# Moving one pool mix ahead of a pool gate's product in the mixer's TensorE order

## The chip, the cores and the metric

The kernel runs on one core of one Trainium2 chip. The metric is the device time of one execution in microseconds, the median over runs. Five engines work side by side: TensorE (PE, with its weight loads PEld), VectorE (DVE), ScalarE (ACT), GpSimd (POOL) and SyncE (SP), which issues most of the transfers.

## The reference, cut to what matters

One block of a network for 256 tokens of width 2048: a feed-forward part (SwiGLU, inner width 5632), a mixer, and a second feed-forward part, each with a norm before and after and a residual. All is float32. The change lies in the mixer:

```python
def _hybrid_mixer(u, ...):
    p = u @ w_in
    z_a, z_b, g_a, g_b = jnp.split(p, IN_SPLITS, axis=-1)
    y_a = _rwkv7_branch(z_a, ...) @ w_proj_a
    y_b = _pool_branch(z_b, pool_w, pool_scale) @ w_proj_b
    m = jax.nn.sigmoid(g_a) * y_a + jax.nn.sigmoid(g_b) * y_b
    return m @ w_out

def _pool_branch(z, pool_w, pool_scale):
    ...                      # four groups of 256 channels, windows 2, 4, 8, 16
    mixed = pooled - zf      # window mean less the value itself
    y = jnp.einsum('bsgc,gcd->bsgd', mixed, pool_w.astype(jnp.float32))
    y = y.reshape(bsz, seq, POOL_WIDTH) * pool_scale.astype(jnp.float32)
    return y.astype(z.dtype)
```

A *pool mix* is one of the four products `mixed[g] @ pool_w[g]` (256 tokens, 256 by 256). A *pool gate* is 512 of the 2048 columns of `g_b`, with its sigmoid.

## The kernel before, in words

**Products.** Each float32 product is made of three passes over halves: a weight tile w is cast to wH on ScalarE (L342), and the rest wL = w - wH is made on VectorE (L343); the activations are halved in the same way, and `mm3` (L364, with the matmuls L366 to L368) adds wH with the high half, wL with the high half, and wH with the low half. Weights come in by SP's queue (`get_w`, L328) in tiles of 128 by 1024 elements, 512 KB, into four buffers, and the halves go into a ring of five pairs. A full tile feeds two steps of k for both halves of the tokens, 12 matmuls of 512 columns. The weights of a pool mix are one tile of 128 by 512 (256 KB), which feeds 12 matmuls of 256 columns (L976).

**The mixer's groups.** TensorE's order in the mixer is written out by hand as a chain of generators:

- `tok_g` (L887) is a product of 512 columns over the 16 (or 8) tiles of k, tokens on the partitions; it holds two of the four PSUM banks of the pool `mm`, one for each half of the tokens (h = 0 and 1), which take turns at every k. `gb_g(c)` is a pool gate made in that way; its two banks are emptied by ScalarE's sigmoid (L1594) into `sgb`. `z_g(hf, ...)` makes columns of r, k or v for one half of the recurrence's heads; ScalarE empties them at L1135. `pb_g(c)` is the product of the pool branch with w_proj_b, which multiplies into `sgb` (L1663); `ga_g(c)` is a gate of the other branch.
- `mix_g(g)` is a pool mix, by `pool_mix` and `ch_g` (L963): channels on the partitions, one bank of the same pool (`mc`). It is emptied in four steps that follow each other, ScalarE (L1789), VectorE (L1790), and the same again for the second half of the channels, into `yb`.
- `chain(hf)` is the recurrence itself for half the heads: many small matmuls, with work on all engines between them. `weave` fills the time between its steps with matmuls of the generator `rest`.

`seq` runs a list of such groups. Before a group empties its banks it lets the next group do its first step (`prime`), so that TensorE has work.

**What sets the order.** In the mixer only TensorE's order is the written one. What ScalarE, VectorE, GpSimd and SP do, and in which order, is set by the framework's scheduler from the program's dependencies, its own model of time and priorities; casts, low halves and evictions have a raised priority (`BOOST`). The banks and the larger buffers are given out in the order in which the scheduler sees them come free. The two feed-forward parts have a planner of their own (`Plan`), on which the change does not touch.

**Around the change.** A first list runs w_in's columns for the LoRA parts, the two halves of the pool columns, k and v of the first half of the heads, `mix_g(0)`, `mix_g(1)`, and r (`z_g(0, 4)`). Then the list of `rest` begins, as the filler of `chain(0)`: the gate `gb_g(1)`, then `mix_g(2)` and `mix_g(3)`, then k for the second half of the heads (`z_g(1, 1)`). The inputs of all four mixes (`mix[g]`, by `pool_window`) are made with the pool columns, well ahead of all of these. In the profile the window of the change is 840 to 895 us.

Of the kernel before, what the change touches and what calls it, by code (L numbers as in the profile page):

```python
# [260 lines left out]
class Block:  # L261
# [1322 lines left out]
    def mixer(s, prm, uT, rs, resid, emit, gpost, reload):  # L1584
# [7 lines left out]
        def ev_sig(dst):  # L1592
            def ev(h, ps):
                nc.scalar.activation(out=dst(h), in_=ps, func=AF.Sigmoid, scale=rs[h])  # L1594
            return ev
# [40 lines left out]
        def z_g(hf, part=0):  # L1636
            for nme, zc in ((("k", 1), ("v", 2), ("r", 0)), (("k", 1),),
                            (("v", 2), ("r", 0)), (("v", 2),), (("r", 0),))[part]:
                z[hf][nme] = s.unit((P, 4, S), F32, "z" + nme)
                c0 = zc * W + hf * 512  # L1640
                yield from s.across(w_in, c0, at, rs, lambda v: s.shift(
                    v, c0 // P, [z[hf][nme][:, i] for i in range(4)]), scratch(hf))
# [12 lines left out]
        def gb_g(c):  # L1655
            sg = sgb[c] = [s.tmp("sgb"), s.tmp("sgb")]
            yield from s.tok_g(w_in, GB + c * 512, at, NKD, ev_sig(lambda h: sg[h]))

        def pb_g(c):
            sg = sgb[c]  # L1660

            def ev_pb(h, ps):
                nc.vector.tensor_tensor(out=sg[h], in0=ps, in1=sg[h], op=ALU.mult)  # L1663
                nc.gpsimd.dma_start(out=msp[c, :, h], in_=sg[h])
            yield from s.tok_g(prm["w_proj_b"], c * 512, at_b, NKW, ev_pb)
# [4 lines left out]
        def scratch(hf=0):  # L1670
            n = next(turn)
            if hf:
                return [s.unit(p="sc") for _ in range(3)]
            return [s.R[(3 * n + i) % 15] for i in range(3)]
# [7 lines left out]
        def mix_g(g):  # L1682
            yield from s.pool_mix(g, mix[g], prm["pool_w"], pT)
# [3 lines left out]
        def ga_g(c):  # L1687
            sg = s.unit((P, 2, 512), F32, "sga")
            sga.append(sg)
            yield from s.tok_g(w_in, GA + c * 512, at, NKD, ev_sig(lambda h: sg[:, h]))  # L1690
# [28 lines left out]
        pair = s.pair_g(prm["w_proj_a"], (0, 512), at_a, NKW, 4, (ev_pa(0), ev_pa(1)))  # L1719

        def rest():
            yield from s.seq([gb_g(1), mix_g(2), mix_g(3), z_g(1, 1), pb_g(0), pb_g(1), z_g(1, 3), z_g(1, 4), gb_g(2), pb_g(2), gb_g(3), pb_g(3)]
                             + [ga_g(c) for c in range(4)])
            for t in pair:
                if t is None:
                    return
                yield t
# [9 lines left out]
        with s.tc.manual_schedule(engines={mybir.EngineType.PE}):  # L1737
            fill = rest()
            for _ in s.seq([s.across(w_in, 3 * W, at, rs, ev_l, scratch(), 288),  pool_g(0), pool_g(1), z_g(0, 1), z_g(0, 3), mix_g(0), mix_g(1), z_g(0, 4)], fill):
                pass  # L1740
            for hf in range(2):
                s.pre_at = PRE_AT[1 + hf]
                weave(chain(hf), fill)
            for _ in fill:
                pass
# [494 lines left out]
```

## Time and profile before

| | before |
|---|---|
| median of 3 runs | 2007.59 us (2006.14 to 2008.42) |
| the profiled execution | 2004.61 us |
| its span, first to last instruction | 2002.9 us |
| TensorE matmuls, busy | 1990.1 us, 99% |
| VectorE, busy | 1815.1 us, 91% |
| ScalarE, busy | 1223.8 us, 61% |
| GpSimd, busy | 406.3 us, 20% |
| mean granted clock of TensorE | 0.998 |

Matmuls are pipelined and their ends are modelled, so the busy share of TensorE says that matmuls follow each other, not that it is at its peak. What a wait costs is read from the distance between the starts of matmuls.

### The profile page before, as it was taken

The page shows a single profiled execution, that of the slowest core. Times are in us where ns is not written, and L with a number is a line of the kernel's source. Part 1 is how long each engine was busy: PE and PEld are TensorE (multiplying, and loading weights), DVE is VectorE, ACT ScalarE, POOL GpSimd, SP SyncE. Part 2 cuts the span into 40 slices and gives each one's busy share as a digit, 9 for nine tenths or more (in the row PEclk, how much of TensorE's full clock was granted, in tenths as well). Part 3 has the DMA queues.
Part 4 walks back from the last instruction along what each step waited for, and adds up shares of the span by engine and source line. Part 5 has one row for each costly group of instructions (what it writes and reads, how often), then busy time and mean ns, then how long its engine had stood idle before and what let it go on. Part 6 is the DMA issues. An engine that isn't in the chain of part 4 may idle for free.

```text
span 2002.9 us, 29049 instructions
## 1 busy us (share of the span) xinstructions
PE 1990.1 (99%) x9903; PEld 1644.6 (82%) x9903; DVE 1815.1 (91%) x2468; ACT 1223.8 (61%) x1631; POOL 406.3 (20%) x745
## 2 busy tenths in 40 slices
PE   9999999999999999999999999999999999999998
PEld 7888888888888888878788788888888888888886
DVE  7999999999999957789689678989999999999997
ACT  7566665666666566675466435575666666666653
POOL 2000001574100114402320111010000115650000
PEclk9999999999999999999999999999999999999999
DMA  9868896987778777757456547769688889897774
GB/s 346 277 208 262 253 265 216 282 269 229 236 223 261 263 202 212 209 164 215 148 170 188 168 159 258 267 227 297 216 248 268 240 271 272 265 265 220 239 255 169
DMA packets 253110, 470.79 MB, mean 235 GB/s; under 512 B 27299, under 2 KB 30752, under 8 KB 252960
## 3 DMA queue, kind: packets, MB, share of 16 engines
q1 hardware_dynamic: 213696, 400.37, 60.6%
q0 software_dynamic: 38976, 68.03, 15.0%
q8 instruction: 78, 1.28, 0.3%
q10 hardware_dynamic: 288, 0.52, 0.1%
q14 instruction: 72, 0.59, 0.1%
HBM read 443.88 MB, written 8.39 MB: 226 GB/s over the span
## 4 chain that ended last, share of the span: by engine, by line
PE 95%; DVE 2%; issue 1%; DMA 1%; ACT 0%; SPq 0%; DVEq 0%; POOLq 0%; POOL 0%; ACTq 0%
PE mm L366 25%; PE mm L368 25%; PE mm L367 25%; PE ms L368 5%; PE ms L367 5%; PE ms L366 5%; PE tr L1014 1%; DMA w<-in_w_out_dram 1%; PE pA L1967 0%; DVE wL L430 0%; DVE wL L681 0%; PE pU L2052 0%; PE pSa L2064 0%; DMA x<-in_x_dram 0%; PE pY L2087 0%
## 5 line engine op out<-in xcount | busy, mean ns | idle before, releaser
L366 PE MATMUL mm<-wH,xH 128*128 128x512 f32 (+1 forms) x2008 | 784.2, 391 | 1.1 <-ACT sgb L1594 0.6
L367 PE MATMUL mm<-wL,xH 128*128 128x512 f32 (+1 forms) x2008 | 779.5, 388 | 0.1
L368 PE MATMUL mm<-wH,xL 128*128 128x512 f32 (+1 forms) x2008 | 779.5, 388 | 0.0
L366 PEld LDWEIGHTS mm<-wH,xH 128*128 128x128 f32 x2008 | 377.1, 188 | 79.9 <-ACT sgb L1594 1.0
L368 PEld LDWEIGHTS mm<-wH,xL 128*128 128x128 f32 x2008 | 377.0, 188 | 78.7 <-DVE xL L1032 1.1
L367 PEld LDWEIGHTS mm<-wL,xH 128*128 128x128 f32 x2008 | 377.3, 188 | 76.2 <-DVE wL L343 0.9
L676 ACT CAST wH<-t 128x1024 fp32r<-128x1024 f32 x244 | 257.0, 1054 | 211.7 <-DVE t L668 97.3
L420 ACT CAST wH<-w 128x1024 fp32r<-128x1024 f32 x293 | 301.7, 1052 | 119.4 <-PE mm L368 98.3
L430 DVE TENSOR_TENSOR wL<-w,wH 128x1024 fp32r<-128x1024 f32 x293 | 349.8, 1217 | 19.3 <-ACT wH L420 17.7
L681 DVE TENSOR_TENSOR wL<-t,wH 128x1024 fp32r<-128x1024 f32 x244 | 293.0, 1216 | 2.4 <-ACT wH L676 1.4
L342 ACT CAST wH<-w 128x1024 fp32r<-128x1024 f32 (+2 forms) x184 | 188.8, 1029 | 173.8 <-PE mm L368 151.9
L343 DVE TENSOR_TENSOR wL<-w,wH 128x1024 fp32r<-128x1024 f32 (+2 forms) x184 | 217.4, 1188 | 84.0 <-ACT wH L342 82.5
L676 ACT CAST wH<-w 128x1024 fp32r<-128x1024 f32 x244 | 199.4, 836 | 119.2 <-PE mm L368 92.1
L681 DVE TENSOR_TENSOR wL<-w,wH 128x1024 fp32r<-128x1024 f32 x244 | 229.0, 949 | 0.1
L1057 POOL DMA_DIRECT2D x<-T x352 | 179.0, 568 | 146.4 <-DVE wL L681 45.6
L654 POOL DMA_DIRECT2D t<-in_ffn_up_dram x47 | 56.7, 1209 | 569.5 <-DVE wL L681 161.6
L367 PE MATMUL ms<-wL,sH 128*128 128x512 f32 x312 | 121.4, 389 | 0.0
L368 PE MATMUL ms<-wH,sL 128*128 128x512 f32 x312 | 121.4, 389 | 0.0
L366 PE MATMUL ms<-wH,sH 128*128 128x512 f32 x312 | 121.4, 389 | 0.0
L668 DVE TENSOR_TENSOR t<-w,t 128x512 f32<-128x512 f32 x122 | 83.2, 682 | 0.2
L664 DVE TENSOR_TENSOR t<-w,t 128x512 f32<-128x512 f32 x122 | 82.8, 683 | 0.1
L659 DVE TENSOR_TENSOR t<-w,w 128x1024 f32<-128x1024 f32 x62 | 75.3, 1217 | 3.8 <-DMA w<-in_ffn_down_dram 3.8
(353 smaller groups left out, 2308.0 us busy)
## 6 DMA issues: line engine op xcount, KB each, us to landing
w<-in_w_in_dram SPq DMA_DIRECT2D x128, 512.0 KB, 4.3
w<-in_ffn_down_dram SPq DMA_DIRECT2D x104, 512.0 KB, 6.3
w<-in_ffn_up_dram SPq DMA_DIRECT2D x94, 512.0 KB, 5.8
w<-in_ffn_gate_dram SPq DMA_DIRECT2D x92, 512.0 KB, 6.6
w<-in_ffn_gate_dram SPq DMA_DIRECT2D x168, 256.0 KB, 5.8
w<-in_ffn_down_dram SPq DMA_DIRECT2D x131, 256.0 KB, 5.0
w<-in_ffn_up_dram SPq DMA_DIRECT2D x117, 256.0 KB, 5.8
t<-in_ffn_up_dram POOLq DMA_DIRECT2D x47, 512.0 KB, 8.1
```

Of the source, the lines that this page charges most:

```text
L342: s.nc.scalar.copy(vH, v)
L343: s.nc.vector.tensor_tensor(out=vL, in0=v, in1=vH.bitcast(F32), op=ALU.subtract)
L366: nc.tensor.matmul(ps, aH, bH, start=start, stop=False, skip_group_check=seeded)
L367: nc.tensor.matmul(ps, aH, bL, start=False, stop=False, skip_group_check=seeded)
L368: nc.tensor.matmul(ps, aL, bH, start=False, stop=stop, skip_group_check=seeded)
L420: nc.scalar.copy(x["H"], x["v"])
L430: nc.vector.tensor_tensor(out=x["L"], in0=x["v"], in1=x["H"].bitcast(F32), op=ALU.subtract)
L664: V.tensor_tensor(out=v["t24"][:, 0], in0=v["a"][:, 0], in1=v["t13"][:, 1], op=ALU.add)
L668: V.tensor_tensor(out=v["t24"][:, 1], in0=v["b"][:, 1], in1=v["t24"][:, 0], op=ALU.add)
L676: nc.scalar.copy(H, src)
L681: V.tensor_tensor(out=L, in0=src, in1=H.bitcast(F32), op=ALU.subtract)
L1057: nc.gpsimd.dma_start(out=x[0][q * 32:q * 32 + 32, i], in_=src[i * 32:i * 32 + 32, q])
```

## The change

`mix_g(2)` moves to the front of the list of `rest`, ahead of the pool gate `gb_g(1)`. `mix_g(3)` stays behind the gate. The instructions are the same in kind and number.

```diff
         def rest():
-            yield from s.seq([gb_g(1), mix_g(2), mix_g(3), z_g(1, 1), pb_g(0), pb_g(1), z_g(1, 3), z_g(1, 4), gb_g(2), pb_g(2), gb_g(3), pb_g(3)]
+            yield from s.seq([mix_g(2), gb_g(1), mix_g(3), z_g(1, 1), pb_g(0), pb_g(1), z_g(1, 3), z_g(1, 4), gb_g(2), pb_g(2), gb_g(3), pb_g(3)]
                              + [ga_g(c) for c in range(4)])
```

## The prediction

> **What bounds the kernel now.** I read the page's busy shares first, then the waits of TensorE, the table by stage around the edited place, and last the timelines of TensorE, VectorE and ScalarE in that stage.
>
> ```profile
> span 2002.9 us, 29049 instructions
> ...
> PE 1990.1 (99%) x9903; PEld 1644.6 (82%) x9903; DVE 1815.1 (91%) x2468; ACT 1223.8 (61%) x1631; POOL 406.3 (20%) x745
> ...
> PE 95%; DVE 2%; issue 1%; DMA 1%; ACT 0%; SPq 0%; DVEq 0%; POOLq 0%; POOL 0%; ACTq 0%
> ```
>
> The last line is the chain that ended last: it is 95% matmul. A change of order adds no matmul, so it can only give back time in which TensorE stands. Where TensorE waits between 700 us and 1240 us (all of the mixer up to w_out) is this whole list:
>
> ```profile
> PE mm L366 <- ACT sgb L1594: 0.6, 1, 0.6
> PE pU L2052 <- DVE R L2077: 0.3, 1, 0.3
> ```
>
> One of its two rows lies at the edit. L1594 is the sigmoid that empties a gate's PSUM bank (gb_g, ga_g). The weight loads of TensorE, asked from 865 to 895 us, show a second kind of wait:
>
> ```profile
> PEld mm L367 <- DVE wL L343: 0.9, 2, 0.5
> ```
>
> So the low half of a weight tile (wL, L343 on VectorE) comes just too late twice. The table by stage (stretch, length, then busy us of PE, PEld, DVE, ACT and POOL, granted clock, DMA share, GB/s) says why:
>
> ```profile
> 850.00:860.00 10.00, 10.00 (x59) 8.64 (x59) 5.64 (x10) 7.70 (x13) 3.69 (x3) 1.00 0.78 221
> ...
> 870.00:880.00 10.00, 9.36 (x45) 7.30 (x44) 9.88 (x17) 7.79 (x15) 0.53 (x1) 1.00 0.29 74
> ```
>
> From 870 us VectorE is full (9.88 of 10) while TensorE is not (9.36); from 850 to 860 us VectorE has 4.36 us to spare. TensorE's timeline (start, length, instruction, and the wait in brackets):
>
> ```profile
> 839.97 0.39 PE L366 MATMUL mm<-wH,xH 128*128 128x512 f32 x1
> ...
> 868.23 0.28 PE L976 MATMUL mc<-mxT,wH 128*128 128x256 f32 x1
> ...
> 870.98 0.28 PE L976 MATMUL mc<-mxT,wH 128*128 128x256 f32 x1
> 871.10 0.40 PE L366 MATMUL mm<-wH,xH 128*128 128x512 f32 x1
> ...
> 871.57 0.40 PE L368 MATMUL mm<-wH,xL 128*128 128x512 f32 x1
> 872.55 0.51 PE L366 MATMUL mm<-wH,xH 128*128 128x512 f32 x1 [0.58 <-ACT sgb L1594]
> 872.89 0.40 PE L367 MATMUL mm<-wL,xH 128*128 128x512 f32 x1
> ...
> 877.00 0.39 PE L367 MATMUL mm<-wL,xH 128*128 128x512 f32 x1
> 877.23 0.39 PE L368 MATMUL mm<-wH,xL 128*128 128x512 f32 x1
> 877.45 0.39 PE L366 MATMUL mm<-wH,xH 128*128 128x512 f32 x1
> 877.90 0.50 PE L367 MATMUL mm<-wL,xH 128*128 128x512 f32 x1
> 878.24 0.39 PE L368 MATMUL mm<-wH,xL 128*128 128x512 f32 x1
> ...
> 890.52 0.39 PE L366 MATMUL mm<-wH,xH 128*128 128x512 f32 x1
> 890.87 0.50 PE L367 MATMUL mm<-wL,xH 128*128 128x512 f32 x1
> 891.21 0.40 PE L368 MATMUL mm<-wH,xL 128*128 128x512 f32 x1
> ```
>
> gb_g(1) begins at 839.97 and ends with the matmul before 868.23; mix_g(2) and mix_g(3) are the mc rows from 868.23 to 870.98, 24 matmuls in 871.10 - 868.23 = 2.87 us, so 1.44 us for each mix; z_g(1, 1) begins at 871.10. A steady step is 877.23 - 877.00 = 0.23 us. Longer steps are the waits: at 871.57, 0.98 - 0.23 = 0.75, and at 872.55, 0.34 - 0.23 = 0.11, together **0.86** (bank); at 877.45 and 877.90, 0.22 + 0.11 = **0.33** (wL); at 890.52 and 890.87, 0.12 + 0.11 = **0.23** (wL). That makes 1.42 us in the whole stage.
>
> **The bank wait.** In the program before, the four PSUM banks of the products go in the order in which they come free: gb_g(1) has banks 0 and 1, mix_g(2) bank 2, mix_g(3) bank 3, and z_g(1, 1) again 0 and 1. Its second half (h = 1) so needs the gate's second bank, which ScalarE empties last:
>
> ```profile
> 870.25 0.70 ACT L1594 ACTIVATE sgb<-mm,rs 128x512 f32<-128x512 f32 x1
> ...
> 871.80 0.69 ACT L1594 ACTIVATE sgb<-mm,rs 128x512 f32<-128x512 f32 x1
> ```
>
> Bank 0 is free at 870.95, bank 1 at 872.49; the matmul follows at 872.55.
>
> **The change, part by part.**
>
> *Matmuls of mix_g(2).* Twelve, 1.44 us, leave 868.23 and stand at 839.97. Nothing is added: z_g(1, 1) still begins at 871.10, since its matmul predecessors are the same set. One more border between 256- and 512-column groups arises (mix_g(2) and mix_g(3) no longer touch); the two steps behind such a border take 871.57 - 871.10 = 0.47 against 2 x 0.227, so it costs under 0.05 us, taken as 0.
>
> *Banks.* mix_g(2) takes the bank that is free longest at 839.97 (that of mix_g(0)), gb_g(1) then the two of z_g(0, 4), and mix_g(3) and z_g(1, 1) find mix_g(1)'s and mix_g(2)'s, both evicted long since, and for h = 1 the *first* bank of gb_g(1). That is needed at 871.10 + 3 x 0.23 = 871.79. If ScalarE keeps the sigmoid at 870.25, it is free at 870.95: no wait. The gate ends 1.44 us later than now, 869.67 plus the drain, which still is before 870.25. Term: -0.86. From the other side: had z_g(1, 1) to take both banks of the gate again, the need for the second at 871.79 would meet its release at 872.49, and the 0.86 stays.
>
> The gate's own start is new: at 839.97 + 1.44 = 841.41 and 842.09 it needs the banks of z_g(0, 4), the later of which is emptied here:
>
> ```profile
> 840.47 0.68 ACT L1135 ACTIVATE R<-mm,rs 128x512 f32<-128x512 f32 x1
> ```
>
> Free at 841.15, with 0.9 us in hand. Term 0.
>
> *Evictions of mix_g(2)* (two on ScalarE L1789, two on VectorE L1790, one after the other). VectorE's place now:
>
> ```profile
> 876.62 2.35 DVE L343 TENSOR_TENSOR wL<-w,wH 128x1024 fp32r<-128x1024 f32 x2
> 878.89 0.48 DVE L1790 SCALAR_TENSOR_TENSOR yb<-mc,cols,yb 128x256 fp32r<-128x256 f32 x1
> ...
> 888.81 0.48 DVE L1790 SCALAR_TENSOR_TENSOR yb<-mc,cols,yb 128x256 fp32r<-128x256 f32 x1
> ...
> 889.60 3.49 DVE L343 TENSOR_TENSOR wL<-w,wH 128x1024 fp32r<-128x1024 f32 x3
> ```
>
> By the order of tiles these two are mix_g(2)'s. Each holds VectorE for up to 0.48 us, so up to 0.96 us leave the full stage and go to 841 to 860, where 4.36 us are free in the second half. They stand ahead of the conversion at 889.60, whose first result the matmul at 890.87 waits for; with 0.96 less, the 0.23 there go, if TensorE arrives no earlier than now. They stand behind the conversion at 876.62, so the wait at 877.90 is not relieved by them. What their new place may cost: VectorE splits the LoRA weights there, and TensorE takes them soon after.
>
> ```profile
> 842.12 1.22 DVE L361 TENSOR_TENSOR wL<-w,wH 128x1024 fp32r<-128x1024 f32 x1 [0.23 <-ACT wH L360]
> 844.84 0.28 PE L1830 MATMUL pw<-lq,wL 128*128 128x256 f32 x1
> ```
>
> 1.50 us in hand. If both pairs went ahead of it, at worst in series on the two engines, 4 x 0.48 = 1.92: a loss of 0.4 at most. I take 0, since all four must meet one 1.2 us stretch for it.
>
> *Weight tile of mix_g(2).* Its transfer (256 KB, L328 on SP), its cast (L342) and its low half (L343, 128x512) move ahead of all eight tiles of gb_g(1), in the ring of five converted tiles too. The stream is far ahead there: gb_g(1)'s second tile is converted at 833.09 + 1.23 = 834.32 and first read at 842.91.
>
> ```profile
> 833.09 1.23 DVE L343 TENSOR_TENSOR wL<-w,wH 128x1024 fp32r<-128x1024 f32 x1 [1.49 <-ACT wH L342]
> 842.91 0.39 PE L367 MATMUL mm<-wL,xH 128*128 128x512 f32 x1
> ```
>
> That is 8.59 us; The mix's tile, half as wide, costs each engine no more than such a conversion, 1.23, so cover remains. It is the only transfer that the move issues: on SP's queue it passes eight of w_in, on POOL's none. At the other end the ring gets looser: a mix's tile holds a slot but feeds TensorE only 1.44 us, and two of them side by side shrink the reach of the ring just before 871.10. With one, the slot for z_g(1, 1)'s third tile (the one late at 877.90) comes free 2.72 - 1.44 = 1.28 us sooner (a full tile is 12 steps of 0.23). But VectorE converts that tile only at 876.62, 4 us after the sigmoids, behind work of the recurrence. So there are two ends. If those two lists stay, TensorE reaches 877.04 instead of 877.90 and waits the gained 0.86 for the same conversion. If the conversion moves up, the 0.33 goes as well.
>
> *Sum.* The ends are 0 and -1.42. I take the bank wait's **-0.9**: it is the one wait that the order itself touches, and I leave the two wL waits as they are, since one may grow and the other shrink by similar amounts. Against the profiled execution, 2004.61 (span 2002.9) becomes 2003.7. The median of the runs, 2007.59, lies 2.98 above it, so the forecast is **2006.7**. That is 0.05%; about 0.2%, or 4.0 us, is what a measurement of this kernel can tell from no change. Further on TensorE stands only in the 0.3 of the second row above, so a gain at 872 is carried along.
>
> **The rivals.**
>
> *A, the wait moves to wL.* Price as above: all of the bank gain is spent at 877.90, and only the relief at 890.87 is left, between -0.23 and 0: 2007.4. For it: VectorE at 9.88 of 10, and a conversion that is already the last to come. Against it: the slot that opens 1.28 us sooner.
>
> *B, the bank wait stays* because z_g(1, 1) is given both of the gate's banks, or ScalarE puts the first sigmoid after 871.79: 2007.6. Against: two banks are free longer. [...]
>
> *C, slower: the moved mix is evicted late.* Its bank is wanted by mix_g(3) or z_g(1, 1). If its last L1790 stays where it is now, at 888.81 + 0.48 = 889.29, z_g(1, 1) stands from 871.10, 18.2 us: 2025.8. It decides from 871.1 on. For it: the first two mixes, run just ahead of z_g(0, 4), 32 x 3 steps of 0.227 (21.8 us) before 839.97, so they end near 818.2. Their last eviction is
>
> ```profile
> 843.26 0.48 DVE L1790 SCALAR_TENSOR_TENSOR yb<-mc,cols,yb 128x256 fp32r<-128x256 f32 x1
> ```
>
> It ends at 843.74, 25.5 us later. Against it: that lag, from 841.4, ends at 866.9, still 4.2 before the need. The lists of ScalarE and VectorE are set anew by the framework's scheduler, so this rival stands for a poor new list too. The granted clock is 1.00 in both stage rows, through the wait of 0.75. [...]
>
> **How the numbers follow.** Forecast 0.50, A 0.22, B 0.12, C 0.13, and 0.03 for faster by over 0.2%, which the 1.42 us of waits here do not hold. Forecast, A and B all lie within 0.2%, so same is 0.84, slower 0.13. The range: down, the 1.42 us and the spread of the three runs below their median (2007.59 - 2006.14 = 1.45) give 2004.7. Up, the spread above it (0.83) and a mild form of C give 2010.5: for the latter I take 2.1 us, the longest wait that the evictions cause now:
>
> ```profile
> 879.41 0.47 ACT L1789 ACTIVATE yb<-mc,cols 128x256 fp32r<-128x256 f32 x1 [2.10 <-DVE yb L1790]
> ```
>
> **What the next profile would show.** Right: no wait of a matmul for L1594 near 872; mc rows near 840 and near 869.7 with 12 matmuls each; the moved L1790 before 860. Rival A: the step before 877.9 longer than 0.45. B: the L1594 row is still there. C: a wait of TensorE for L1790. The forecast is wrong in size if any wait over 1 us appears between 840 and 1240, since every instruction list but TensorE's is made anew for the whole kernel.

## The result and the profile after: 0.13% slower, nearly all of it at one place

| | before | after |
|---|---|---|
| median of 22 runs each | 2005.8 us (2004.84 to 2008.42) | 2008.46 us (2007.2 to 2010.52) |
| ratio after to before | | 1.0013, 95% interval 1.0007 to 1.0019 |
| span of the profiled execution | 2002.9 us | 2007.3 us |

The ratio makes 2.6 us (1.4 to 3.8). The forecast was a gain of 0.9; the change costs instead: little, but the whole interval lies above 1. The page after shows the same work as before:

```profile
span 2007.3 us, 29049 instructions
...
PE 1989.7 (99%) x9903; PEld 1643.1 (82%) x9903; DVE 1816.7 (91%) x2468; ACT 1223.9 (61%) x1631; POOL 407.8 (20%) x745
```

The number of matmuls is the same, so the loss is time in which TensorE stands. The waits of TensorE from 700 to 1240 us (waiting instruction, what it waits for, us in total, times, longest) were two rows before; now there are five, of which these are new:

```profile
PE mm L366 <- ACT wH L342: 1.5, 1, 1.5
PE mm L367 <- DVE wL L343: 0.9, 1, 0.9
PE pn L1877 <- issue: 0.5, 1, 0.5
...
PE pA L1967 <- ACT R L1959: 0.3, 1, 0.3
```

The row for L1594 (the sigmoid) of before is not among the five. The first two are one place, where mix_g(2) ends and gb_g(1) begins. TensorE's timeline after:

```profile
842.46 0.28 PE L976 MATMUL mc<-mxT,wL 128*128 128x256 f32 x1
842.58 0.28 PE L976 MATMUL mc<-mxT,wH 128*128 128x256 f32 x1
844.35 0.50 PE L366 MATMUL mm<-wH,xH 128*128 128x512 f32 x1 [1.49 <-ACT wH L342]
845.81 0.50 PE L367 MATMUL mm<-wL,xH 128*128 128x512 f32 x1 [0.95 <-DVE wL L343]
846.14 0.40 PE L368 MATMUL mm<-wH,xL 128*128 128x512 f32 x1
```

The reader takes the starts: 844.35 - 842.58 = 1.77 where a mix's step is 0.12; 845.81 - 844.35 = 1.46 and 846.14 - 845.81 = 0.33 where a step is 0.227. Above the steady steps that is 1.65 + 1.23 + 0.11 = **2.99 us**: the gate's first weight tile comes too late, first its cast, then its low half.

To count the whole change, three matmuls serve as marks in TensorE's timeline: the first of z_g(0, 4), the first of pb_g(1), and the last of the program. Before, then after:

```profile
818.18 0.40 PE L366 MATMUL mm<-wH,xH 128*128 128x512 f32 x1
...
914.21 0.40 PE L366 MATMUL mm<-wH,yb 128*128 128x512 f32 x1
...
1993.16 0.39 PE L368 MATMUL mm<-kH,xL 128*128 128x512 f32 x1
```

```profile
819.48 0.40 PE L366 MATMUL mm<-wH,xH 128*128 128x512 f32 x1
...
918.64 0.39 PE L366 MATMUL mm<-wH,yb 128*128 128x512 f32 x1
...
1997.57 0.39 PE L368 MATMUL mm<-kH,xL 128*128 128x512 f32 x1
```

From z_g(0, 4) to pb_g(1) it was 96.03 us and is 99.16; from there to the end 1078.95 and 1078.93. How steady such a distance is, the traces of four of the experiments below show: from pb_g(1) to the end, where their order is that of before, they have 1078.87 to 1078.92. So the change costs **3.1 us**, all within these 96 us. The spans differ by 4.4, but 819.48 - 818.18 = 1.30 of that arises before the change is reached, in the wait for the first input (TensorE's waits up to 60 us, before and after):

```profile
PE tr L1014 <- DMA x<-in_x_dram: 0.4, 1, 0.4
```

```profile
PE tr L1014 <- DMA x<-in_x_dram: 1.7, 1, 1.7
```

**Why the tile is late.** ScalarE's timeline before, with the casts of weight tiles (L342), the eviction of z_g(0, 4) (L1135) and the cast of the LoRA weights (L360):

```profile
829.29 1.05 ACT L342 CAST wH<-w 128x1024 fp32r<-128x1024 f32 x1 [1.58 <-PE mm L368]
832.01 1.05 ACT L342 CAST wH<-w 128x1024 fp32r<-128x1024 f32 x1 [1.67 <-PE mm L368]
...
841.04 1.04 ACT L360 CAST wH<-w 128x1024 fp32r<-128x1024 f32 x1
```

And after:

```profile
830.59 0.62 ACT L342 CAST wH<-w 128x512 fp32r<-128x512 f32 x1 [1.58 <-PE mm L368]
...
840.79 0.69 ACT L1135 ACTIVATE R<-mm,rs 128x512 f32<-128x512 f32 x1 [3.82 <-PE mm L368]
...
841.74 0.69 ACT L1135 ACTIVATE R<-mm,rs 128x512 f32<-128x512 f32 x1
842.31 1.05 ACT L360 CAST wH<-w 128x1024 fp32r<-128x1024 f32 x1
843.24 2.95 ACT L342 CAST wH<-w 128x1024 fp32r<-128x1024 f32 x3
```

At the end of z_g(0, 4) `prime` lets the next group do its first step, and with it its first load. Only then does the program of `chain(0)` ask for its LoRA weights (`split_w`), which take one pair of the same ring of five. Before, the group that was let ahead was the gate, whose first load is two full tiles, 24 matmuls or 24 x 0.227 = 5.4 us of work for TensorE. After, it is mix_g(2), whose only load is the half tile cast at 830.59, 1.44 us of work. The gate's tiles now come behind the LoRA tile. That tile's cast carries no raised priority and stands in ScalarE's list behind the eviction of z_g(0, 4), which waits for TensorE until 840.79. So the gate's cast begins at 843.24, and its low half follows on VectorE:

```profile
843.39 1.23 DVE L361 TENSOR_TENSOR wL<-w,wH 128x1024 fp32r<-128x1024 f32 x1 [0.18 <-ACT wH L360]
844.53 3.49 DVE L343 TENSOR_TENSOR wL<-w,wH 128x1024 fp32r<-128x1024 f32 x3
```

TensorE was through with mix_g(2) near 842.7. The LoRA transfer itself is in by about 836 (an estimate, 829.79 + 1.04 + 5.2, from POOL's last issue of it and the median from issue to landing):

```profile
829.79 1.04 POOL L1823 DMA_DIRECT2D w<-in_rwkv_a_dram  x2
```

```profile
w<-in_rwkv_a_dram POOLq DMA_DIRECT2D x2, 128.0 KB, 5.2
```

Its pair of the ring is free by then too: in x3_lora_sp below, with the same order of groups, this cast begins at 832.95 (an estimate for after, since it is read in another run). So from 836 to 842.31, some 6 us, it is the place in the list that holds the cast. ScalarE does not take the cast first here: it is idle for 3.82 us ahead of the eviction at 840.79, and the cast, with its data in, begins only behind the evictions, at 842.31.

**What stands beside it.** The bank wait that the change was to remove is smaller, not gone:

```profile
876.72 0.39 PE L368 MATMUL mm<-wH,xL 128*128 128x512 f32 x1
877.11 0.50 PE L366 MATMUL mm<-wH,xH 128*128 128x512 f32 x1
877.45 0.40 PE L367 MATMUL mm<-wL,xH 128*128 128x512 f32 x1
```

```profile
876.38 1.26 ACT L1594 ACTIVATE sgb<-mm,rs 128x512 f32<-128x512 f32 x2
```

(0.39 - 0.23) + (0.34 - 0.23) = 0.27 in place of 0.86: -0.59. The two wL waits of 0.33 and 0.23 are gone from z_g(1, 1) but for a step longer by 0.09 (at 884.97): -0.47. New beside the 2.99 are the pn row (853.73 - 852.87, 0.64 above a step) and the pA row (0.47). Together 2.99 - 0.59 - 0.47 + 0.64 + 0.47 = 3.04 of 3.1; what is left lies in the recurrence's small matmuls, some of which take longer (by the starts, pA 0.43 us and pV 0.14) and some less (pB 0.57).

### The profile page after: what moved, and what is told of

Its sections match the earlier page's. It is cut to its first block, busy times and chain, and to the rows that moved or that the text cites. A ratio compares the mean times of both kernels' runs of the same rounds, so it can differ in the third digit from the quotient of the medians.

```text
span 2007.3 us, 29049 instructions
## 1 busy us (share of the span) xinstructions
PE 1989.7 (99%) x9903; PEld 1643.1 (82%) x9903; DVE 1816.7 (91%) x2468; ACT 1223.9 (61%) x1631; POOL 407.8 (20%) x745
## 4 chain that ended last, share of the span: by engine, by line
PE 90%; DVE 4%; DMA 2%; issue 2%; ACT 1%; POOL 0%; SPq 0%; DVEq 0%; POOLq 0%; ACTq 0%
PE mm L366 24%; PE mm L368 24%; PE mm L367 23%; PE ms L367 5%; PE ms L368 5%; PE ms L366 5%; DMA w<-in_ffn_down_dram 1%; PE tr L1014 1%; DVE wL L681 1%; DVE wL L430 1%; DMA w<-in_w_out_dram 0%; PE pA L1967 0%; DVE t L659 0%; DVE wL L343 0%; DMA R<-R 0%
## 5 line engine op out<-in xcount | busy, mean ns | idle before, releaser
L342 ACT CAST wH<-w 128x1024 fp32r<-128x1024 f32 (+2 forms) x184 | 188.7, 1029 | 174.4 <-PE mm L368 148.7
L343 DVE TENSOR_TENSOR wL<-w,wH 128x1024 fp32r<-128x1024 f32 (+2 forms) x184 | 217.6, 1189 | 80.9 <-ACT wH L342 79.3
```

Source lines behind the costliest of these rows:

```text
L342: s.nc.scalar.copy(vH, v)
L343: s.nc.vector.tensor_tensor(out=vL, in0=v, in1=vH.bitcast(F32), op=ALU.subtract)
```

## The experiments

My theory, called the ring (P in the expectations): the loss is the first load that `prime` sends ahead of the LoRA tile, half a tile in place of two tiles. Rivals: the mix in front of the gate costs by its own conversion and evictions, which crowd ScalarE and VectorE (Q), or by the banks (R); or the place of the LoRA transfers on POOL's queue is the cause. A loss of 3 us is 0.15%, and the intervals below are some 0.1% wide to each side: by time each of the runs is the same as before, and what is said of causes rests on the traces, one for each kernel. All distances from the same marks:

| kernel | time, us | ratio to before, interval | z_g(0, 4) to end, us | against before |
|---|---|---|---|---|
| before (profile) | 2005.4 beside these runs | | 1174.98 | 0 |
| after (profile) | | 1.0013 (1.0007 to 1.0019) | 1178.09 | +3.11 |
| x1_two | 2006.64 | 1.0005 (0.9995 to 1.0014) | 1175.70 | +0.72 |
| x1_one | 2006.28 | 1.0005 (0.9996 to 1.0013) | 1176.07 | +1.09 |
| x2_before_one | 2005.84 | 1.0001 (0.9993 to 1.0010) | 1176.08 | +1.10 |
| x3_lora_sp | 2007.10 | 1.0008 (0.9999 to 1.0017) | 1176.72 | +1.74 |

**x1_two: the changed order, with the gate's first two tiles sent ahead again.**

```diff
-            for k, wH, wL in s.load_w(w, k0, min(kstep, KT - k0), c0, cw):     # ch_g
+            tiles = s.load_w(w, k0, min(kstep, KT - k0), c0, cw)
+            if ahead:
+                ahead()                  # mix_g(2): early[1] = s.load_w(w_in, 0, 4, GB + 512, 512)
+            for k, wH, wL in tiles:
...
+            got = list(first) if k0 == 0 else []                               # tok_g
+            tiles = got + s.load_w(w, k0 + len(got), min(n, KT - k0) - len(got), c0, cw)
```

> TensorE's order is that of the changed kernel; only the first two weight tiles of gb_g(1) are loaded and converted together with mix_g(2)'s tile, so that they stand in the ring ahead of the LoRA weights of chain(0). Theory P (ring): in the changed kernel the LoRA tile, which ScalarE casts only behind the eviction of z_g(0, 4), stands ahead of the gate's tiles, and TensorE has only a half tile of mix_g(2) to work on meanwhile. By P the waits for L342 and L343 near 842 to 846 us (2.99 us) and the one before pn go, and the freed bank's gain stays: 0.5 to 1.4 us below the kernel before, ratio 0.9993 to 0.9998. Rival Q (crowding): the moved mix's own conversion and evictions crowd ScalarE and VectorE at 840 to 860 us; the waits stay, ratio 1.001 or more. Rival R (banks): the gate, now 1.44 us later, waits for the banks of z_g(0, 4); a wait for L1135 shows, ratio 1.0005 or more.

ScalarE's casts in x1_two:

```profile
836.09 1.05 ACT L342 CAST wH<-w 128x1024 fp32r<-128x1024 f32 x1 [1.67 <-PE mm L368]
...
842.82 1.05 ACT L360 CAST wH<-w 128x1024 fp32r<-128x1024 f32 x1
```

The LoRA cast is even later than after, 842.82, and it does no harm: the gate's tiles are cast ahead of it, and no wait for L342 or L343 is left in the list from 700 to 1240 us. So the 2.99 goes whole, with the mix still in front of the gate and converted and evicted there, which speaks against rival Q; the distance falls by 2.4, from +3.11 to +0.72. The measured 1.0005 still lies above the 0.9993 to 0.9998 that I had forecast, though its interval reaches into them. What costs is a short wait ahead of mix_g(2), whose bank (mix_g(0)'s, by the order of the evictions) is emptied at 841.54 by L1800 (L1790 of before), and the bank wait, which I had expected to go:

```profile
841.10 0.39 PE L368 MATMUL mm<-wH,xL 128*128 128x512 f32 x1
841.60 0.39 PE L981 MATMUL mc<-mxT,wH 128*128 128x256 f32 x1
...
874.70 0.50 PE L366 MATMUL mm<-wH,xH 128*128 128x512 f32 x1 [0.98 <-ACT sgb L1599]
```

```profile
871.99 2.09 ACT L1929 ACTIVATE R<-R,oka,cols 128x256 f32<-128x256 f32 x4
873.97 1.26 ACT L1599 ACTIVATE sgb<-mm,rs 128x512 f32<-128x512 f32 x2
```

The first is 0.50 - 0.23 = 0.27 and 0.10 on the step behind it, the second 1.14 and 0.11 on the step behind it, against 0.86 before. The two wL waits (0.56) are absent here too, and a pA group of the recurrence takes 2.02 us (892.08 to 894.10) where it took 1.41 before: 0.37 + 1.25 - 0.86 - 0.56 + 0.61 = 0.81, near the 0.72. Rival R has a part in that: the wait for a bank is there, though not for L1135, which it named. z_g(1, 1) does get the gate's first bank, but both sigmoids now stand behind four instructions of the recurrence, where before they stood among these four. The bank was right; the place in the list is set by the scheduler.

**x1_one: the same with one tile** (`early[1] = s.load_w(w_in, 0, 2, GB + 512, 512)`).

> As x1_two, but only one of the gate's tiles (k = 0, 1) stands ahead of the LoRA tile. Theory P: the second one is cast right behind the LoRA cast, near 843.2 us, and its low half is ready near 845.5, about when TensorE wants it (841.3 + 1.44 + 2.72 = 845.5): a wait of 0 to 0.5 us, ratio 0.9995 to 1.0002, between x1_two and the changed kernel. Rival Q: the waits stay, ratio 1.001 or more. Rival R: as in x1_two.

```profile
PE mm L366 <- ACT sgb L1599: 1.0, 1, 1.0
PE mm L367 <- DVE wL L343: 0.4, 1, 0.4
```

With one tile the gate begins without a wait, and the wait comes 2.7 us later, at its second tile, and is small, if a little over the 0 to 0.5 that I expected. So the loss goes with how much work is sent ahead: half a tile of a mix alone, 2.99; one gate tile more, 0.66 (847.19 - 846.41 = 0.78 for 0.23, and 0.11 on the next step); two, none.

**x2_before_one: the order of before, with the gate's first load cut to one tile.**

```diff
-        for k0 in range(0, KT, n):
-            for k, wH, wL in s.load_w(w, k0, min(n, KT - k0), c0, cw):
+        for k0 in ((0, 2) if one else ()) + tuple(range(4 if one else 0, KT, n)):
+            nk = 2 if one and k0 < 4 else min(n, KT - k0)
+            for k, wH, wL in s.load_w(w, k0, nk, c0, cw):
...
+            yield from s.tok_g(w_in, GB + c * 512, at, NKD, ev_sig(lambda h: sg[h]), one=c == 1)
```

> The kernel before, with the gate first and both mixes behind it; only the first load of gb_g(1) brings one tile (k = 0, 1) in place of two, so that its second tile falls behind the LoRA tile. No mix is moved. Theory P: that tile is cast near 842.5 to 843.5 us and its low half ready near 844.7 to 845.8, where TensorE wants it at 842.7: a wait of 2 to 3 us, ratio 1.0010 to 1.0015, as large as the change's loss. Rivals Q and R: nothing is crowded and no bank is taken later, ratio 1.0000.

```profile
842.95 0.39 PE L368 MATMUL mm<-wH,xL 128*128 128x512 f32 x1
843.54 0.50 PE L366 MATMUL mm<-wH,xH 128*128 128x512 f32 x1 [0.20 <-ACT wH L342]
844.99 0.50 PE L367 MATMUL mm<-wL,xH 128*128 128x512 f32 x1 [0.95 <-DVE wL L343]
845.33 0.40 PE L368 MATMUL mm<-wH,xL 128*128 128x512 f32 x1
```

With no mix moved, the same two waits appear (wH and wL, at 843.54 and 844.99), behind the LoRA cast as in the changed kernel, and TensorE loses 0.36 + 1.22 + 0.11 = 1.7 us in them. That is less than the 2 to 3 us that I expected, and the ratio of 1.0001 lies below the 1.0010 to 1.0015 that I had forecast; its interval is too wide to resolve 1.7 us. The marks give +1.10, since a wait of 1.1 in the recurrence (pV, L1898) comes on top and the bank wait of 0.86, among others, is absent here. So a wait of this kind needs no moved mix.

**x3_lora_sp: the changed order, with the LoRA weights on SP's queue** (`nc.sync.dma_start` for `G.dma_start` in `fill_l`).

> TensorE's order and the ring's order are those of the changed kernel; only the small LoRA transfers (L1823) are issued by SP in place of POOL, for both halves of the heads, whereupon the scheduler lists the LoRA cast and the casts of gb_g(1) ahead of the eviction of z_g(0, 4) on ScalarE. Theory P: the gate's first tiles are cast before 840 us, the waits near 842 to 846 us go, ratio 0.9993 to 1.0000. Rivals Q and R: the mix's work and the banks are as in the changed kernel, the waits stay, ratio 1.001 or more.

```profile
832.95 1.05 ACT L360 CAST wH<-w 128x1024 fp32r<-128x1024 f32 x1 [2.10 <-PE mm L368]
835.67 1.05 ACT L342 CAST wH<-w 128x1024 fp32r<-128x1024 f32 x1 [1.67 <-PE mm L368]
```

```profile
PE mc L976 <- ACT R L1135: 1.1, 1, 1.1
PE mm L366 <- ACT sgb L1594: 1.0, 1, 1.0
```

The scheduler puts the LoRA cast before the eviction, at 832.95, the gate's casts follow, and the waits for L342 and L343 are gone. So the LoRA tile's late place in ScalarE's list is what held the gate's. The run is still 1.74 behind, because its banks are dealt out otherwise: mix_g(2) gets z_g(0, 4)'s first bank and waits for its eviction, which costs 1.38 with the step behind it, and z_g(1, 1) waits 1.26 for the sigmoid. The rival of POOL's queue is so not refuted but a part of the cause: the loss needs both, the gate's tiles behind the LoRA tile and the LoRA cast late in the list, and with the transfers on POOL the scheduler put it there. Why it did is not shown. Nor does the run separate the ring's order from the priority of the casts: in every version here the gate's casts keep to the order of the ring, and a kernel with a raised priority for the LoRA cast alone was not run.

**x4_mix_early: the mixes put elsewhere, so that `prime` meets the gate.**

```diff
-... z_g(0, 1), z_g(0, 3), mix_g(0), mix_g(1), z_g(0, 4)], fill)
+... z_g(0, 1), mix_g(0), z_g(0, 3), mix_g(1), mix_g(2), z_g(0, 4)], fill)
...
-[mix_g(2), gb_g(1), mix_g(3), z_g(1, 1), ...
+[gb_g(1), mix_g(3), z_g(1, 1), ...
```

> The list before r (z_g(0, 4)) becomes z_g(0, 1), mix_g(0), z_g(0, 3), mix_g(1), mix_g(2), z_g(0, 4), and the list of rest begins with gb_g(1), mix_g(3), z_g(1, 1). So mix_g(2) is out of the place between gate and z_g(1, 1), as in the changed kernel, but what the end of z_g(0, 4) sends ahead of the LoRA weights is again the gate's first load, two full tiles. Theory (the ring): the waits for L342 and L343 between 840 and 847 us, 2.99 in the changed kernel, are gone, and z_g(1, 1), whose second half finds the gate's first bank, waits less than the 0.86 of before. From z_g(0, 1)'s first matmul to pb_g(1)'s first matmul it is 142.42 us in the kernel before and 145.55 in the changed one; the theory expects 141.5 to 142.5, and a time of 2004.5 to 2005.5 beside 2005.4 of before. Rival (the mix ahead of the gate costs by its own evictions and bank, wherever it stands): some 3 us remain, 144.5 to 146. A second rival is a held bank: z_g(0, 4) or the gate waits for L1790 of one of the three mixes near 820 or 840, each us of it added to the 142.

```profile
833.76 1.05 ACT L342 CAST wH<-w 128x1024 fp32r<-128x1024 f32 x1 [1.67 <-PE mm L368]
...
843.16 1.05 ACT L360 CAST wH<-w 128x1024 fp32r<-128x1024 f32 x1
```

```profile
PE pA L1967 <- ACT R L1959: 1.2, 2, 0.9
PE pV L1897 <- DVE n L1880: 0.8, 1, 0.8
PE mm L366 <- ACT sgb L1594: 0.4, 1, 0.4
```

The gate's tiles are again cast ahead of the LoRA tile and TensorE runs through 840 to 847 without a gap, mix_g(2) out of the way all the same. That part of the theory held, and 142.44 us from z_g(0, 1) to pb_g(1) lies where it expected it. The time did not: 2007.17 beside 2005.39, ratio 1.0008 (0.9999 to 1.0017), and from z_g(0, 1) to the end 1224.11 against 1221.37 us. My mark was badly chosen, since with one mix less in `rest` the recurrence and the filler meet at other places, and pb_g(1) comes earlier in the recurrence; so the 142.44 proves little. The 2.7 us are mostly other waits: 0.3 for the bank of mix_g(2) at 818 (the held bank of the second rival, small), the first two rows above, and at 1290 us, far from the edit, a wait for L748 that grew from 0.5 to 1.5:

```profile
1292.28 0.47 PE L366 MATMUL mm<-wH,xH 128*128 128x512 f32 x1 [1.50 <-DVE u L748]
```

No version here beats before. None of the five measured ratios or times lies in the range that the theory forecast, though several intervals reach into it; what came each time as forecast was whether the waits at the gate's first tiles are there. Each new order removes a wait that can be named and draws others of 0.3 to 1.4 us from the new lists of ScalarE and VectorE.

## Why the prediction was wrong, point by point

- *What bounds the kernel*: "it can only give back time in which TensorE stands" left out that a new order can make TensorE stand anew. With the same 9903 matmuls TensorE now stands 2.99 us more at one place.
- *Weight tile of mix_g(2)*: this is the step of the sum that failed. It took the lead of the conversions in the trace of before, 8.59 us for the gate's second tile, as a property of the stage ("the stream is far ahead there"), and charged the moved tile against it. It counted which transfers that tile passes on the queues, and not the LoRA tile, which takes a pair of the same ring. But the lead belonged to just two tiles, those that `prime` sent ahead of the LoRA tile, and the change moved these two behind it. Taken as 0, it measured 2.99. Both facts stood in the view: after the casts at 829.29 and 832.01 the next weight cast of before is L360 at 841.04, a hole of 8 us.
- *Matmuls and banks*: right. The banks were dealt out as described, and no matmul step of the border costs.
- *The bank wait*: the direction was right, the size -0.59 for -0.86. "If ScalarE keeps the sigmoid at 870.25" was the condition, and it did not hold: the gate ended later by the 2.99 beside the 1.44 foreseen, and the sigmoids came as a pair at 876.38. In x1_two, without the 2.99, the sigmoids still move back, to 873.97, and the wait is 1.25, so in that run the -0.9 did not come either.
- *Evictions of mix_g(2)*: right at 0. They end well before the 871.1 from which rival C decides:

```profile
868.45 0.48 DVE L1790 SCALAR_TENSOR_TENSOR yb<-mc,cols,yb 128x256 fp32r<-128x256 f32 x1 [0.72 <-ACT yb L1789]
```

- *The two wL waits*, left as they were in the sum: all but 0.09 of the 0.56 is gone, while the pn and pA waits of 1.11 came. TensorE reached z_g(1, 1)'s third tile at 882.02 in place of 877.45, 4.57 us later, which by itself gives the conversions time; no run separates that.
- *A gain at 872 is carried along*: right in kind, for the loss. From pb_g(1) on, the two kernels differ by 0.02 us in 1079.
- *The rivals*: none of A, B and C came about as a mechanism. C had the direction, and its sentence on a poor new list comes nearest, but it named late evictions and a wait for L1790, and there is none. What came was the last sentence of the prediction's text, a wait over 1 us between 840 and 1240.
- *The numbers*: that 2008.46 lies in the range of 2004.7 to 2010.5 is luck, since its upper end was made of the spread of three runs and a wait of 2.1 us for evictions. The start of the forecast was off too: 2007.59 was the median of three runs, and that of 22 is 2005.8, so the 2.98 added to the profiled execution was 1.8 too much.
- *The clock*: the longest stand at the edit is 1.65 us; the stage row after shows TensorE standing 2.4 us in all at a granted clock of 1.00.

```profile
840.00:850.00 10.00, 7.56 (x42) 6.23 (x41) 6.41 (x8) 7.49 (x10) 6.18 (x13) 1.00 0.46 140
```

## What to carry to other kernels

Where a group sends its first load ahead of another user of the same buffers, ask how much work that load is, in us of the engine that waits, and not only how early it is: here a smaller group in its place, 1.44 us of work for 5.4, let TensorE stand 2.99 us. Before counting on a lead, look in the list of the converting engine for the next instruction behind the last tile that has it, and for what that instruction waits. And read small changes between marks in the trace: here two marks gave 3.1 us where the spans differ by 4.4 and the medians by 2.6.

## What the runs showed beside that

The same program start, untouched by the change, took from 0.4 to 1.7 us of waiting for the first transfer of x in the two profiled executions, so spans of single executions can't be compared within a microsecond. In each of the cases seen here the 512-column step behind a wait is some 0.1 us longer than steady (0.30 to 0.34 for 0.227), and so are steps behind a group of the recurrence's small matmuls without any wait (in the kernel before, 892.96 - 892.62 = 0.34). A wait therefore costs more than its own row says: the bank wait of before has a row of 0.6, and by the starts of the matmuls it cost 0.86.
